# Preparing the operands of the gate and up projections in smaller pieces, placed by a time allowance on VectorE

## The chip, the cores and the metric

The kernel runs on one core of a Trainium2 chip. Its time is the device time of one execution in microseconds (us); of several runs the median is given. TensorE (PE) multiplies, VectorE (DVE) and ScalarE (ACT) work elementwise, GpSimd (POOL) and SyncE (SP) issue transfers. Each engine works through its own queue in order.

## The reference

One encoder layer: retention and windowed attention, an output projection, a LayerNorm, a SwiGLU feed-forward network with a gated embedding, and a second LayerNorm. The change is in the feed-forward network, whose matrices are 1024 x 2816 (gate, up) and 2816 x 1024 (down), for 1024 tokens in float32:

```python
h = _layer_norm(ALPHA * h + mix, ln1_gain[i], ln1_bias[i])
g = jnp.einsum('bsd,df->bsf', h, w_ffn_gate[i])
up = jnp.einsum('bsd,df->bsf', h, w_ffn_up[i])
ffn = jnp.einsum('bsf,fd->bsd', jax.nn.silu(g) * up, w_ffn_down[i])
```

## The kernel before, in words

Every float32 operand is split into a high and a low half in a reduced format (`split`, L70 to L72): ScalarE writes the high half, VectorE then subtracts it to get the low half. A product is three matmuls for each contraction tile (`mm3c`, L783 to L785): high by high, high by low, low by high.

The gate and up projections multiply 2 x 2 blocks by seven products instead of eight. The 2816 hidden columns make eleven pairs of 128-wide tiles (`Pair`, n = 0 to 10). A pair is worked through for m = 0 (gate) and m = 1 (up), and each product p of a half is one unit, written p/m below: twelve matmuls of 512 columns. Its weights are an input block or a sum of blocks (`raw` and `ln` are the loaded blocks, the sums stand in a tile named `H`), which `Pair.prep` computes and splits into one of eight operand slots (`w` and `u` tiles in the trace). The token side is prepared once for all pairs.

From pair 2 on, product 2 of both halves is taken together and is itself made of seven products of half the size, in three fine parts: F0 (products 1, 6, 5), F1 (7, 2) and F2 (4, 3), with 18, 12 and 12 matmuls of 256 columns. They share two banks, so F1 may write only when the three additions of F0's results (`post_fine`, L1295) are done. The order of units on TensorE is 1/0, 1/1, F0, 6/0, F1, 6/1, F2, 5/0, 5/1, 7/0, 7/1, 4/0, 4/1, 3/0, 3/1.

Products 1, 6, 7 and 4 of a half accumulate in one bank. Behind 1, 6 and 7 the bank is copied out by ScalarE (L1352, L1354, L1359) before the next of them may add to it. Behind 4/1 VectorE multiplies and makes three sums (L1367, L1335), behind 7 and 3 it adds (L1346), ScalarE takes the Silu (L1329) and VectorE multiplies (L1331).

All engines run in the order in which the program is written. The main loop issues unit k's matmuls, its evictions, and then `ahead(2, ...)`, which prepares operands of units up to eight further on, as long as operand slots are free:

```python
for k in range(NG):
    gunits[k][1]()
    gunits[k][2]()
    if k in (8, 11, 16, 19):
        fine.pop(0)()
    ahead(2, k + 1 + min(8, 4 + k))
```

One preparation is one piece. For product 5 it is the split and then the two sums for products 7 and 3 (L1234, L1235); for product 6 the two sums for 6 and 5 (L1227, L1228) and the split; for F0 two sums (L1243) and four splits. Slots that are short set how many preparations stand behind a unit. Loads of the next pair's weights (L1219) are issued behind the preparations of products 5 and 4.

Of the kernel before, what the change touches and what calls it, by code (L numbers as in the profile page):

```python
# [12 lines left out]
ALU = mybir.AluOpType  # L13
# [29 lines left out]
def layer(tc, xT, xn, w_first, w_mt, w_rv, w_out, w_pg, w_pe, pT, w_gu, w_dn,  # L43
          consts, dec_b, dec_c, sink, gng, lnp, out):
    nc = tc.nc
    act, dve, pool, pe, sp = nc.scalar, nc.vector, nc.gpsimd, nc.tensor, nc.sync
# [12 lines left out]
    def nm(s):  # L59
        uid[0] += 1  # L60
        return f"{s}{uid[0]}"
# [8 lines left out]
    def split(raw, hi, lo):  # L70
        act.activation(hi, raw, AF.Copy)  # L71
        dve.tensor_tensor(lo, raw, hi.bitcast(F32), ALU.subtract)  # L72
# [8 lines left out]
    def behind(ins):  # L81

        tc.add_manual_dep(ins.ins, recent[0], mybir.DependencyInfo(
            mybir.DependencyClass.NoSync, mybir.DependencyReason.DATA), reason="order")
        return ins

    last = {}
# [33 lines left out]
    def a_tile(shape, name, tag=None, dt=F32):  # L121

        turnA[0] += tag is None
        return big.tile(list(shape), dt, tag=tag or f"A{turnA[0] % 2}", bufs=4, name=nm(name))
# [8 lines left out]
    def bt(shape, tag, bufs=None, dt=F32):  # L133
        return bpool.tile(list(shape), dt, tag=tag, bufs=bufs, name=nm(tag))
# [15 lines left out]
    with tc.manual_schedule(engines={mybir.EngineType.DVE, mybir.EngineType.SP}):  # L150
        for kt in range(KT):
# [26 lines left out]
            w = wf[kt % 2]  # L178
# [81 lines left out]
    for h in range(2):  # L260
        sl = slice(h * HF, (h + 1) * HF)
        b = st[1, h]
        for g in range(2):
            a = slice(64 * g, 64 * g + 64)
# [123 lines left out]
    class Retention:  # L388


        def __init__(self, i, y, states):
            self.i, self.y, self.states = i, y, states
            self.rk, self.dq, _ = pairs[i]
            self.U = [bt([P, NT - 1, 64], f"kv{d}") for d in range(2)]
            self.kdec, self.pt, self.qq, self.r = {}, {}, {}, {}
            self.qd, self.dt = decays[i]
# [184 lines left out]
    def put(x, o, dst):  # L581
        behind(act.activation(o[:, 0, :], x, AF.Copy))
        behind(dve.tensor_tensor(o[:, 1, :], x, o[:, 0, :].bitcast(F32), ALU.subtract))
        sp.dma_start(dst, o.bitcast(F32))
# [85 lines left out]
    def ytile(k):  # L670
        if ys[k] is None:
            ys[k] = a_tile([P, S], "y", "A0" if k < 4 else "A1")
        return ys[k]
# [46 lines left out]
    with tc.manual_schedule(engines={mybir.EngineType.PE}):  # L720
# [7 lines left out]
        a = Attention(0, ytile(1))  # L728
# [11 lines left out]
        Q, X = (lambda q: (r.scores, q)), (lambda q: (r.turn, q))  # L740
# [4 lines left out]
        for i in range(1, NPAIR):  # L745
# [3 lines left out]
            a = Attention(i, ytile(2 * i + 1))  # L749
            if i == 2:  # L750
                late = [ytile(6), ytile(7)]
                op = twin(late[1].bitcast(F32R))
                side.extend(presplit_out(2, [op], 2, 3.5, late[:1]))
                side.extend(presplit_small(0, op, 30) + presplit_small(1, op, 38))
            elif i == 3:
                op = twin(bt([P, S], "aq", 3, F32R))
# [15 lines left out]
    def ct(shape, tag, bufs=None, dt=F32):  # L772
        return cpool.tile(list(shape), dt, tag=tag, bufs=bufs, name=nm(tag))
# [175 lines left out]
    part = ct([P, 8, HF], "h0b")  # L949
# [169 lines left out]
    for k in range(4):  # L1119
        c = slice(k * P, (k + 1) * P)  # L1120
# [43 lines left out]
    Q = HF // 2  # L1164
# [3 lines left out]
    oslots = []  # L1168
    fright, fsum = {}, []
# [5 lines left out]
    def take_op():  # L1175
        return oslots.pop(0)
# [32 lines left out]
    class Pair:  # L1209


        def __init__(self, n):
            self.n = n
            self.raw, self.ops, self.bank, self.ev, self.s = {}, {}, {}, {}, {}

        def load(self, m, part=(0, 1)):
            for i in part:
# [2 lines left out]
                for j in range(2):  # L1220
                    self.raw[m, i, j] = r[:, j * HF:(j + 1) * HF]

        def prep(self, p, m):
            a = lambda i, j: self.raw[m, i, j]
            s = self.s.setdefault(m, [sarena[:, 4 * m + k, :] for k in range(4)])
            if p == 6:
                dve.tensor_tensor(s[1], a(1, 0), a(1, 1), ALU.add)  # L1227
                dve.tensor_tensor(s[0], s[1], a(0, 0), ALU.subtract)  # L1228
            src = {1: lambda: a(0, 0), 2: lambda: a(0, 1), 4: lambda: a(1, 1), 5: lambda: s[1], 6: lambda: s[0],
                   7: lambda: s[2], 3: lambda: s[3]}[p]()  # L1230
            t = self.ops[p, m] = take_op()
            split(src, t[:, 0, :], t[:, 1, :])
            if p == 5:
                dve.tensor_tensor(s[2], a(0, 0), a(1, 0), ALU.subtract)  # L1234
                dve.tensor_tensor(s[3], a(0, 1), s[0], ALU.subtract)  # L1235

        def prep_fine(self, part):

            x, y = (self.raw[m, 0, 1] for m in range(2))
            left = {1: x[:, :Q], 2: x[:, Q:], 4: y[:, Q:], 5: fsum[0], 6: fsum[1], 7: fsum[2], 3: fsum[3]}  # L1240

            def sum_(q, a, b, op):
                dve.tensor_tensor(left[q], a, b, op)  # L1243

            def put(t, h, q):
                c = slice(h * Q, (h + 1) * Q)
                split(left[q], t[:, 0, c], t[:, 1, c])
                self.fine[q] = t, h * Q

            if part == 0:  # L1250
                self.fine = {}
                t, u, v = (take_op() for _ in range(3))
                self.fu = u
                sum_(5, y[:, :Q], y[:, Q:], ALU.add)
                sum_(6, left[5], x[:, :Q], ALU.subtract)
                split(x, t[:, 0, :], t[:, 1, :])
                self.fine.update({1: (t, 0), 2: (t, Q)})
                put(u, 0, 5)
                put(v, 0, 6)
            elif part == 1:  # L1260
                sum_(7, x[:, :Q], y[:, :Q], ALU.subtract)
                put(self.fu, 1, 7)
            else:
                w = take_op()
                sum_(3, x[:, Q:], left[6], ALU.subtract)
                put(w, 0, 4)
                put(w, 1, 3)

        def mm_fine(self, part):

# [110 lines left out]
    NP = NHID // 2  # L1381
    gunits = []
    pairs2 = [Pair(n) for n in range(NP)]

    def g_unit(n, p, m, k):
        pr = pairs2[n]

        def prep():
            pr.prep(p, m)
            if n + 1 < NP and p in (5, 4):  # L1390
                pairs2[n + 1].load(m, ((0,), (1,))[p == 4])

        return prep, lambda: pr.mm(p, m), lambda: pr.post(p, m, k), 1

    def f_unit(n, part):
        pr = pairs2[n]
        return lambda: pr.prep_fine(part), lambda: pr.mm_fine(part), lambda: pr.post_fine(part), (3, 0, 1)[part]

    for n in range(NP):
        for p in (1, 6, 5, 7, 4, 3) if n >= FROM else (1, 2, 6, 5, 7, 4, 3):  # L1400
# [12 lines left out]
    n = 0  # L1413
    for k, upto in enumerate((2, 4, 8, 12)):
        c = slice(k * P, (k + 1) * P)
# [35 lines left out]
    def arenas_a():  # L1451
        arena("a", rawt(2 * HF).rearrange("p (a b) -> p a b", a=2), 2)
        arena("a", rawt(2 * HF).rearrange("p (a b) -> p a b", a=2), 2)
        for _ in range(2):
            arena("a", ct([P, 2, HF], "ln", 2), 2)

    def op_arena(t, n=4):
        arena("op", t, n)
# [195 lines left out]
    dunits = []  # L1654
# [36 lines left out]

    NG, ND = len(gunits), len(dunits)
    ln2 = []
    done = [0, 0, 0]

    def ahead(what, upto):

        units = gunits if what == 2 else dunits
        while done[what] < min(upto, len(units)) and (what < 2 or units[done[2]][3] <= len(oslots)):
            units[done[what]][what % 2]()  # L1700
            done[what] += 1

    def load_ln2():
        for j in range(2):
            g = ct([P, D], "u", 4)
            sp.dma_start(g, lnp[2 + j].partition_broadcast(P))
            ln2.append(g)
# [19 lines left out]
    with tc.manual_schedule(engines={ET.PE, ET.DVE, ET.Activation, ET.Pool, ET.SP}):  # L1727
        for _ in range(4):
            oslots.append(wp.tile([P, 2, HF], F32R, tag="w", bufs=4, name=nm("w")))
            oslots.append(ct([P, 2, HF], "u", 4, F32R))  # L1730
        fine = fine_right(RIGHT[2])
        evs.extend(a_tile([P, 2, HF], "ev") for _ in range(7))
        fsum.extend([cst[:, 0:Q], cst[:, Q:2 * Q], cst[:, 2 * Q:3 * Q], ct([P, Q], "fs", 1)])
        ahead(2, 4)
        for k in range(NG):
            gunits[k][1]()
            gunits[k][2]()
            if k in (8, 11, 16, 19):
                fine.pop(0)()
            ahead(2, k + 1 + min(8, 4 + k))  # L1740
            while stores and stores[0][0] <= k:
                stores.pop(0)[1]()
            j = k + 1 - NG
            if j == -6:
                arenas_a()
                op_arena(ct([P, 4, 2, HF], "h0a", dt=F32R))
                op_arena(big16((P, 4, 2, HF)))
                op_arena(big16((P, 4, 2, HF)))
                arena("chain", ct([P, 8, HF], "h0b"), 8)
            if j == -4:  # L1750
                op_arena(big16((P, 4, 2, HF)))
                arena("b", big.tile([P, 8, HF], F32, tag="H", bufs=4, name=nm("H")), 8)
            if j >= -6:
                ahead(0, j + 7)
            if j >= -4:
                ahead(1, j + 5)
        arena("chain", ct([P, 8, HF], "h2"), 8)
        op_arena(ct([P, 4, 2, HF], "h3", dt=F32R), 4)
        rings["op"] += [ct([P, 2, HF], "u", 4, F32R) for _ in range(2)]
        for k in range(ND):  # L1760
            d_step(k)
# [85 lines left out]
```

## Time and profile before

| | us |
|---|---|
| median of 3 runs (lowest, highest) | 1214.11 (1213.49, 1217.27) |
| profiled execution | 1212.36 |
| its span, first to last instruction | 1210.6 |
| TensorE busy | 1171.8 (97%) |
| VectorE busy | 844.7 (70%) |
| ScalarE busy | 570.6 (47%) |
| gate and up stage | about 540 to 992 |

The profile lists one execution. Times are us from the span's start. A timeline row has start, length, engine, line, operation, tiles written <- read, shapes, and in brackets the idle time of the engine before it with what ended it. Each tile's buffer number is left out there. The line number is that of the code that issued the instruction, so the halves of all splits have L71 and L72, and matmuls of this stage L783 to L785. Banks are called `bmm`, `bs`, `bt` and `bo`, evicted results `ev`, the fine sums `cst` and `fs`. "Clock" is the share of TensorE's full clock that was granted.

### The profile page before, as it was taken

How to read it: one execution, taken by the hardware profiler on the slowest of the kernel's cores; microseconds unless marked ns; L12 is line 12 of the kernel's file. 1: busy time of each engine (PE TensorE's matmuls, PEld its weight loads, DVE VectorE, ACT ScalarE, POOL GpSimd, SP SyncE). 2: the span in 40 equal slices, each digit the busy share in tenths (PEclk: the TensorE clock that was granted, in tenths of full speed). 3: DMA queues.
4: the chain of work that ended last, by engine and by line, in shares of the span. 5: the costliest groups of instructions: out<-in, count | busy, mean ns of one | idle time of the engine just before them, and what ended most of it. 6: DMA issues, size and time to landing. Idle time of an engine off the chain costs nothing.

```text
span 1210.6 us, 17418 instructions
## 1 busy us (share of the span) xinstructions
PE 1171.8 (97%) x6230; PEld 975.4 (81%) x6230; DVE 844.7 (70%) x1571; ACT 570.6 (47%) x1133; POOL 120.2 (10%) x181
## 2 busy tenths in 40 slices
PE   9999999999999999999989988988998899999997
PEld 7888888888888888888878777877877788888885
DVE  5565777867758879667876667667666765765677
ACT  5665348676754364124433333334334344552463
POOL 2001021111100220000000000000000011124232
PEclk9999999999999999999999999999999999999999
DMA  7346647454457747662321241323133169999977
GB/s 253 99 155 239 232 155 266 156 191 151 155 216 248 284 173 285 206 228 82 131 98 76 87 131 62 112 88 131 44 108 109 70 186 342 355 238 212 260 172 208
DMA packets 80662, 211.73 MB, mean 175 GB/s; under 512 B 9536, under 2 KB 14784, under 8 KB 80576
## 3 DMA queue, kind: packets, MB, share of 16 engines
q1 hardware_dynamic: 71936, 193.84, 45.7%
q0 software_dynamic: 8640, 16.78, 7.9%
q8 instruction: 49, 0.80, 0.3%
q14 instruction: 37, 0.30, 0.1%
HBM read 139.29 MB, written 62.13 MB: 166 GB/s over the span
## 4 chain that ended last, share of the span: by engine, by line
PE 82%; DVE 12%; ACT 3%; issue 2%; DMA 0%; ACTq 0%; DVEq 0%; SPq 0%
PE bmm L77 6%; PE bmm L79 6%; PE bmm L78 6%; PE bt L783 5%; PE bt L785 5%; PE bt L784 5%; PE bmm L783 4%; PE bmm L785 4%; PE bmm L784 4%; PE bs L783 4%; PE bs L785 4%; PE bs L784 4%; PE bo L783 4%; PE bo L785 4%; PE bo L784 4%; DVE ev L1335 2%
## 5 line engine op out<-in xcount | busy, mean ns | idle before, releaser
L77 PE MATMUL bmm<-H,w 128*128 128x512 f32 x240 | 97.2, 405 | 0.2 <-ACT H L71 0.2
L79 PE MATMUL bmm<-H,w 128*128 128x512 f32 x240 | 94.1, 392 | 0.0
L78 PE MATMUL bmm<-H,w 128*128 128x512 f32 x240 | 94.0, 392 | 0.0
L1472 POOL DMA_DIRECT2D h0b<-in_w_dn x24 | 21.6, 902 | 576.5 <-DVE h0a L72 543.9
L72 DVE TENSOR_TENSOR w<-H,w 128x512 fp32r<-128x512 f32 x48 | 33.1, 690 | 31.9 <-ACT w L71 31.9
L77 PEld LDWEIGHTS bmm<-H,w 128*128 128x128 f32 x240 | 45.1, 188 | 10.1 <-ACT H L71 0.9
L79 PEld LDWEIGHTS bmm<-H,w 128*128 128x128 f32 x240 | 45.0, 188 | 10.0
L72 DVE TENSOR_TENSOR w<-raw,w 128x512 fp32r<-128x512 f32 x52 | 35.7, 692 | 24.4 <-ACT w L71 24.2
L78 PEld LDWEIGHTS bmm<-H,w 128*128 128x128 f32 x240 | 45.2, 188 | 7.8
L71 ACT ACTIVATE w<-H 128x512 fp32r<-128x512 f32 x48 | 30.1, 627 | 36.0 <-DVE H L1228 33.3
L71 ACT ACTIVATE u<-H 128x512 fp32r<-128x512 f32 x43 | 27.0, 628 | 41.9 <-DVE H L1228 29.6
L535 ACT ACTIVATE sc<-sc,st 128x385 f32<-128x385 f32 (+1 forms) x64 | 37.2, 585 | 17.1 <-DVE st L533 16.9
L71 ACT ACTIVATE w<-raw 128x512 fp32r<-128x512 f32 x52 | 32.1, 626 | 20.3 <-PE bmm L79 6.9
L531 DVE CUSTOM_DVE_ANT_0 sc<-cst,bs,skb 128x384 f32<-128x384 f32 (+1 forms) x64 | 34.9, 574 | 9.2 <-PE bs L530 7.9
L1329 ACT ACTIVATE ev<-ev 128x512 f32<-128x512 f32 x33 | 20.9, 633 | 36.9 <-DVE ev L1346 27.1
L72 DVE TENSOR_TENSOR u<-H,u 128x512 fp32r<-128x512 f32 x43 | 29.5, 686 | 9.4 <-ACT u L71 9.4
L72 DVE TENSOR_TENSOR u<-raw,u 128x512 fp32r<-128x512 f32 (+1 forms) x30 | 18.3, 608 | 25.4 <-ACT u L71 25.4
L541 ACT ACTIVATE sc<-sc,st 128x384 f32<-128x384 f32 (+1 forms) x64 | 34.0, 580 | 0.8 <-DVE st L539 0.8
L71 ACT ACTIVATE H<-ln 128x512 fp32r<-128x512 f32 (+1 forms) x34 | 22.9, 677 | 24.1 <-DMA ln<-ad 7.5
L526 POOL COPY sc<-skb 128x1 f32<-128x1 f32 x64 | 15.7, 253 | 182.1 <-PE bt L553 157.2
L72 DVE TENSOR_TENSOR H<-ln,H 128x512 fp32r<-128x512 f32 (+1 forms) x34 | 25.0, 746 | 8.4 <-ACT H L71 8.3
L1335 DVE TENSOR_TENSOR ev<-ev,ev 128x512 f32<-128x512 f32 x44 | 29.5, 690 | 1.1
(914 smaller groups left out, 3790.7 us busy)
## 6 DMA issues: line engine op xcount, KB each, us to landing
ad<-ev SPq DMA_DIRECT2D x33, 512.0 KB, 3.4
pgd<-pro SPq DMA_DIRECT2D x28, 512.0 KB, 3.0
raw<-in_w_gu SPq DMA_DIRECT2D x22, 512.0 KB, 4.0
ln<-in_w_gu SPq DMA_DIRECT2D x22, 512.0 KB, 4.2
raw<-ad SPq DMA_DIRECT2D x40, 256.0 KB, 5.8
ln<-ad SPq DMA_DIRECT2D x37, 256.0 KB, 6.4
H<-in_w_dn SPq DMA_DIRECT2D x33, 256.0 KB, 7.2
wod<-aq SPq DMA_DIRECT2D x15, 512.0 KB, 2.7
```

The source lines that it names most:

```text
L71: act.activation(hi, raw, AF.Copy)
L72: dve.tensor_tensor(lo, raw, hi.bitcast(F32), ALU.subtract)
L77: pe.matmul(o, lh, rh, start=start, stop=False)
L78: pe.matmul(o, lh, rl, start=False, stop=False)
L79: recent[0] = pe.matmul(o, ll, rh, start=False, stop=stop).ins.name
L531: dve.tensor_tensor_reduce(sc[g][:, :nk], cst[:, tc0:tc0 + nk], b[:, :nk], slope(i, g), skb[:, 2 * i + g:2 * i + g + 1], ALU.add, ALU.max, ...
L535: act.activation(sc[g][:, :nk + 1], sc[g][:, :nk + 1], AF.Exp, bias=st_[:, 1, j, g:g + 1], accum_out=st_[:, 2, j, g:g + 1])
L541: behind(act.activation(sc[g][:, :nk], sc[g][:, :nk], AF.Copy, scale=st_[:, 3, j, g:g + 1]))
L783: pe.matmul(o, lh, rh, start=start, stop=False, skip_group_check=True)
L784: pe.matmul(o, lh, rl, start=False, stop=False, skip_group_check=True)
L785: pe.matmul(o, ll, rh, start=False, stop=stop, skip_group_check=True)
L1335: dve.tensor_tensor(self.ev[dst][:, 0, :], left, right, op)
```

## The change

A preparation is no longer one piece. Each unit now has a list of items, and each item the number of operand slots it takes, a time for VectorE, and a function. The sums of products 6 and 5 become items of their own (`Pair.sums`), and the fine parts fall into sums, the split of the whole block and single splits; the sum for fine product 7 is made with the other sums. Each unit also carries the time of its matmuls (2.72, or 2.16, 1.44, 1.44 for the fine parts) and the time that VectorE's evictions behind it take (`after`, or 1.45). `ahead_g` puts behind unit k only items that fit in the time of unit k + 1 less the evictions of unit k and less what earlier items overdrew, except that an item of unit k + 1 always goes. The look-ahead is nine units instead of eight. Evictions, matmuls and the order of units stay.

```diff
-        def prep(self, p, m):
+        def sums(self, p, m):
             a = lambda i, j: self.raw[m, i, j]
             s = self.s.setdefault(m, [sarena[:, 4 * m + k, :] for k in range(4)])
             if p == 6:
                 dve.tensor_tensor(s[1], a(1, 0), a(1, 1), ALU.add)
                 dve.tensor_tensor(s[0], s[1], a(0, 0), ALU.subtract)
+            else:
+                dve.tensor_tensor(s[2], a(0, 0), a(1, 0), ALU.subtract)
+                dve.tensor_tensor(s[3], a(0, 1), s[0], ALU.subtract)
+
+        def prep(self, p, m):
...
             t = self.ops[p, m] = take_op()
             split(src, t[:, 0, :], t[:, 1, :])
-            if p == 5:
-                dve.tensor_tensor(s[2], a(0, 0), a(1, 0), ALU.subtract)
-                dve.tensor_tensor(s[3], a(0, 1), s[0], ALU.subtract)
...
+            def sums():
+                x, y = xy()
+                dve.tensor_tensor(fsum[0], y[:, :Q], y[:, Q:], ALU.add)
+                dve.tensor_tensor(fsum[1], fsum[0], x[:, :Q], ALU.subtract)
+                dve.tensor_tensor(fsum[2], x[:, :Q], y[:, :Q], ALU.subtract)
+
+            def whole():
+                t = take_op()
+                split(xy()[0], t[:, 0, :], t[:, 1, :])
+                f.update({1: (t, 0), 2: (t, Q)})
...
+            def last():
+                x, y = xy()
+                dve.tensor_tensor(fsum[3], x[:, Q:], fsum[1], ALU.subtract)
+                put(4, y[:, Q:])
+                put(3, fsum[3], 4)
+
+            return [[(0, 1.1, sums), (1, 0.62, whole), (1, 0.36, lambda: put(6, fsum[1])), (1, 0.36, lambda: put(5, fsum[0]))],
+                    [(0, 0.36, lambda: put(7, fsum[2], 5))], [(1, 1.1, last)]][part]
...
     def g_unit(n, p, m, k):
         pr = pairs2[n]
 
+        def sums():
+            pr.sums(p, m)
+            if n + 1 < NP and p == 5:
+                pairs2[n + 1].load(m, (0,))
+
         def prep():
             pr.prep(p, m)
-            if n + 1 < NP and p in (5, 4):
-                pairs2[n + 1].load(m, ((0,), (1,))[p == 4])
-
-        return prep, lambda: pr.mm(p, m), lambda: pr.post(p, m, k), 1
+            if n + 1 < NP and p == 4:
+                pairs2[n + 1].load(m, (1,))
+
+        items = [(1, 0.62, prep)]
+        if p == 6:
+            items.insert(0, (0, 1.24, sums))
+        elif p == 5:
+            items.append((0, 1.24, sums))
+        after = {2: (0.62, 1.24), 7: (0.62, 1.24), 4: (0, 2.5), 3: (0.62, 1.9)}.get(p, (0, 0))[m]
+        return items, lambda: pr.mm(p, m), lambda: pr.post(p, m, k), 2.72, after
 
     def f_unit(n, part):
         pr = pairs2[n]
-        return lambda: pr.prep_fine(part), lambda: pr.mm_fine(part), lambda: pr.post_fine(part), (3, 0, 1)[part]
+        return pr.prep_fine(part), lambda: pr.mm_fine(part), lambda: pr.post_fine(part), (2.16, 1.44, 1.44)[part], 1.45
...
+    items = [(u, *x) for u, g in enumerate(gunits) for x in g[0]]
+    debt = [0.0]
+
+    def ahead_g(k, upto):
+
+        units = [g[3] for g in gunits] + [2.72]
+        room = units[k + 1] - gunits[k][4] - debt[0] if k >= 0 else 100.0
+        while items and items[0][0] < upto and items[0][1] <= len(oslots) and (items[0][2] <= room or items[0][0] <= k + 1):
+            room -= items[0][2]
+            items.pop(0)[3]()
+        debt[0] = max(0.0, -room)
...
             if k in (8, 11, 16, 19):
                 fine.pop(0)()
-            ahead(2, k + 1 + min(8, 4 + k))
+                debt[0] += 2.2
+            ahead_g(k, k + 1 + min(9, 4 + k))
```

From pair 2 on the items behind each unit are the same in every pair: behind 3/0 the split of 6/0 and the last small split of F1; behind 3/1 nothing; behind 1/0 the sums and the split of 6/1; behind 1/1 F2's items and the split of 5/0; behind F0 the gate half's sums for 7 and 3; behind 6/0 the split of 5/1; behind F1 the up half's sums; behind 6/1 the splits of 7/0 and 7/1; behind F2 those of 4; behind 5/0 those of 3 and the next pair's 1/0; behind 5/1 the next 1/1 and the next fine sums; then the other fine splits one behind each of 7/0, 7/1 and 4/0, with the sums for the next 6/0 behind 4/0; behind 4/1 nothing.

On VectorE, pair 3, from F2's last small halves to F0's additions, the rows before were (`raw_5893` and `raw_5913` are the first weight blocks of the gate and up half, `w_5321` holds 5/0 and `u_5322` 5/1):

```order
L72 TENSOR_TENSOR u_5320<-fs_5337,u_5320 128x256
L72 TENSOR_TENSOR w_5321<-H_4542,w_5321 128x512
L1234 TENSOR_TENSOR H_4542<-raw_5893,ln_5973 128x512
L1235 TENSOR_TENSOR H_4542<-raw_5893,H_4542 128x512
L72 TENSOR_TENSOR u_5322<-H_4542,u_5322 128x512
L1234 TENSOR_TENSOR H_4542<-raw_5913,ln_5977 128x512
L1235 TENSOR_TENSOR H_4542<-raw_5913,H_4542 128x512
L1295 TENSOR_TENSOR ev_5336<-ev_5335,bmm_6198 128x256
L1295 TENSOR_TENSOR ev_5336<-ev_5335,bmm_6198 128x512
L1295 TENSOR_TENSOR ev_5336<-ev_5336,bmm_6198 128x256
```

The same place in the changed kernel, where L1300 is the additions, L1230 and L1231 the sums, and `raw_5931`, `raw_5965` the two blocks:

```order
L72 TENSOR_TENSOR u_5320<-fs_5337,u_5320 128x256
L72 TENSOR_TENSOR w_5321<-H_4542,w_5321 128x512
L1300 TENSOR_TENSOR ev_5336<-ev_5335,bmm_6188 128x256
L1300 TENSOR_TENSOR ev_5336<-ev_5335,bmm_6188 128x512
L1300 TENSOR_TENSOR ev_5336<-ev_5336,bmm_6188 128x256
L1230 TENSOR_TENSOR H_4542<-raw_5931,ln_6002 128x512
L1231 TENSOR_TENSOR H_4542<-raw_5931,H_4542 128x512
L72 TENSOR_TENSOR u_5322<-H_4542,u_5322 128x512
```

Four sums and the low half of 5/1 moved from in front of F0's additions to behind them.

On ScalarE, the same pair, around the copies of 1/0 and 1/1 (L1352), before (`w_5323` holds 6/0, `w_5319` 6/1, `w_5321` 5/0, `u_5318` the last fine piece of F1 and `u_5320` the two of F2):

```order
L71 ACTIVATE w_5323<-H_4542 128x512
L71 ACTIVATE u_5318<-cst 128x256
L1329 ACTIVATE ev_5333<-ev_5333 128x512
L71 ACTIVATE w_5319<-H_4542 128x512
L71 ACTIVATE u_5320<-raw_5913 128x256
L71 ACTIVATE u_5320<-fs_5337 128x256
L1352 ACTIVATE ev_5335<-bs_6157 128x512
L71 ACTIVATE w_5321<-H_4542 128x512
L1352 ACTIVATE ev_5335<-bs_6177 128x512
```

And in the changed kernel, where the copies are L1357, the Silu L1334 and the first fine piece lies in `w_5317`:

```order
L1334 ACTIVATE ev_5333<-ev_5333 128x512
L71 ACTIVATE w_5323<-H_4542 128x512
L71 ACTIVATE w_5317<-cst 128x256
L1357 ACTIVATE ev_5335<-bs_6148 128x512
L71 ACTIVATE w_5319<-H_4542 128x512
L1357 ACTIVATE ev_5335<-bs_6166 128x512
L71 ACTIVATE u_5320<-raw_5965 128x256
L71 ACTIVATE u_5320<-fs_5337 128x256
L71 ACTIVATE w_5321<-H_4542 128x512
```

The split of 6/1 moved between the two copies, and F2's two small splits, the second of which reads `fs`, moved behind both.

More of the change, by code (lines that the diff above doesn't have):

```diff
@@ L1213, in __init__ @@
             self.n = n
-            self.raw, self.ops, self.bank, self.ev, self.s = {}, {}, {}, {}, {}
+            self.raw, self.ops, self.bank, self.ev, self.s, self.fine = {}, {}, {}, {}, {}, {}
         def load(self, m, part=(0, 1)):
@@ L1228, in prep @@
                 dve.tensor_tensor(s[0], s[1], a(0, 0), ALU.subtract)
+            else:
+                dve.tensor_tensor(s[2], a(0, 0), a(1, 0), ALU.subtract)
+                dve.tensor_tensor(s[3], a(0, 1), s[0], ALU.subtract)
+        def prep(self, p, m):
+            a = lambda i, j: self.raw[m, i, j]
+            s = self.s.get(m)
             src = {1: lambda: a(0, 0), 2: lambda: a(0, 1), 4: lambda: a(1, 1), 5: lambda: s[1], 6: lambda: s[0],
@@ L1232, in prep @@
             split(src, t[:, 0, :], t[:, 1, :])
-            if p == 5:
-                dve.tensor_tensor(s[2], a(0, 0), a(1, 0), ALU.subtract)
-                dve.tensor_tensor(s[3], a(0, 1), s[0], ALU.subtract)
         def prep_fine(self, part):
[L1239 to L1243, printed above, removed]
@@ L1245, in put @@
-            def put(t, h, q):
-                c = slice(h * Q, (h + 1) * Q)
[L1247 to L1267, printed above, removed]
+            f = self.fine
@@ new lines, in xy @@
+            def xy():
+                return [self.raw[m, 0, 1] for m in range(2)]
+            def sums():
[7 more added lines that the diff above has]
+                f.update({1: (t, 0), 2: (t, Q)})
@@ new lines, in put @@
+            def put(q, src, beside=None):
+                t, h = (f[beside][0], 1) if beside else (take_op(), 0)
+                c = slice(h * Q, (h + 1) * Q)
+                split(src, t[:, 0, c], t[:, 1, c])
+                f[q] = t, h * Q
+            def last():
[5 more added lines that the diff above has]
+                    [(0, 0.36, lambda: put(7, fsum[2], 5))], [(1, 1.1, last)]][part]
@@ L1693, in layer @@
     ln2 = []
-    done = [0, 0, 0]
+    done = [0, 0]
     def ahead(what, upto):
-        units = gunits if what == 2 else dunits
-        while done[what] < min(upto, len(units)) and (what < 2 or units[done[2]][3] <= len(oslots)):
-            units[done[what]][what % 2]()
+        while done[what] < min(upto, len(dunits)):
+            dunits[done[what]][what]()
             done[what] += 1
+    items = [(u, *x) for u, g in enumerate(gunits) for x in g[0]]
[7 more added lines that the diff above has]
+        debt[0] = max(0.0, -room)
     def load_ln2():
@@ L1733, in layer @@
         fsum.extend([cst[:, 0:Q], cst[:, Q:2 * Q], cst[:, 2 * Q:3 * Q], ct([P, Q], "fs", 1)])
-        ahead(2, 4)
+        ahead_g(-1, 4)
         for k in range(NG):
```

## The prediction

> **What bounds the kernel now.** The page comes first: TensorE (PE) is busy for nearly the whole span.
>
> ```profile
> PE 1171.8 (97%) x6230; PEld 975.4 (81%) x6230; DVE 844.7 (70%) x1571; ACT 570.6 (47%) x1133; POOL 120.2 (10%) x181
> ```
>
> So only the missing 3% and the clock are to be had, and the question is where they lie. The table by stage (columns: length, then busy time of PE, PEld, VectorE (DVE), ScalarE (ACT), POOL, then granted clock, DMA share and GB/s) puts the end of pairs 0 and 1 of the gate and up stage, a steady later pair, and two pairs with a spell of halved clock beside each other:
>
> ```profile
> 569.00:611.00 42.00, 42.00 (x187) 34.74 (x186) 33.38 (x54) 17.18 (x32) 0.00 (x0) 1.00 0.28 94
> 652.40:693.80 41.40, 38.27 (x187) 32.04 (x187) 28.11 (x50) 15.28 (x28) 0.00 (x0) 1.00 0.28 95
> 693.80:736.80 43.00, 39.91 (x187) 33.25 (x187) 28.10 (x50) 15.27 (x28) 0.00 (x0) 0.96 0.28 93
> 714.30:717.70 3.40, 3.40 (x12) 2.73 (x11) 2.64 (x5) 0.87 (x2) 0.00 (x0) 0.50 0.74 261
> 861.00:904.00 43.00, 39.87 (x187) 33.23 (x186) 28.13 (x51) 15.28 (x28) 0.00 (x0) 0.96 0.28 92
> ```
>
> In the later pairs PE is idle some 3.1 us of every 41.4, while VectorE is busy for 28.1 and ScalarE for 15.3 of it: neither is short of time, so somebody's place in a queue is wrong. Line 783, the first matmul of each product, tells who is waited for (the count of 18 is 9 weight loads and 9 matmuls, one of each in the nine pairs 2 to 10):
>
> ```profile
> its engine sat idle before it (us, times) until:
>   DVE ev L1295: 48.4, 18
>   ACT ev L1352: 13.3, 18
> ```
>
> The timeline of pair 3 shows both waits, and the pace of PE without them:
>
> ```profile
> 652.23 0.39 PE L783 MATMUL bt<-h,w 128*128 128x512 f32 x1
> 654.95 0.39 PE L783 MATMUL bt<-h,u 128*128 128x512 f32 x1
> ...
> 663.11 0.28 PE L783 MATMUL bmm<-h0b,w 128*128 128x256 f32 x1
> 665.09 0.42 ACT L71 ACTIVATE u<-fs 128x256 fp32r<-128x256 f32 x1 [2.90 <-DVE fs L1243]
> 665.14 0.28 PE L785 MATMUL bmm<-sg,u 128*128 128x256 f32 x1
> 665.42 0.58 ACT L1352 ACTIVATE ev<-bs 128x512 f32<-128x512 f32 x1
> 665.89 0.62 ACT L71 ACTIVATE w<-H 128x512 fp32r<-128x512 f32 x1
> 666.05 0.50 PE L783 MATMUL bs<-H,w 128*128 128x512 f32 x1 [0.63 <-ACT ev L1352]
> ...
> 668.67 0.39 PE L785 MATMUL bs<-H,w 128*128 128x512 f32 x1
> 669.10 0.60 ACT L1354 ACTIVATE ev<-bs 128x512 f32<-128x512 f32 x1 [0.51 <-PE bs L785]
> 671.56 0.39 PE L783 MATMUL bmm<-fine,u 128*128 128x256 f32 x1 [2.50 <-DVE ev L1295]
> ```
>
> Wait A, 0.63: product 6 of the gate half (6/0) adds to the bank of 1/0, so 1/0 must be copied out first (L1352). ScalarE would copy it some 5 us earlier, but stands 2.90 behind a small split whose input `fs` VectorE has not yet computed. Wait B, 2.50: the second fine part (F1) needs the three additions L1295 of F0. F0's last matmul began at 665.14, and VectorE came to them only at 670.17, because these stood ahead of them in its queue:
>
> ```profile
> 666.55 0.69 DVE L72 TENSOR_TENSOR w<-H,w 128x512 fp32r<-128x512 f32 x1 [0.58 <-ACT w L71]
> 667.16 0.68 DVE L1234 TENSOR_TENSOR H<-raw,ln 128x512 f32<-128x512 f32 x1
> 667.76 0.69 DVE L1235 TENSOR_TENSOR H<-raw,H 128x512 f32<-128x512 f32 x1
> 668.36 0.68 DVE L72 TENSOR_TENSOR u<-H,u 128x512 fp32r<-128x512 f32 x1
> 668.96 0.68 DVE L1234 TENSOR_TENSOR H<-raw,ln 128x512 f32<-128x512 f32 x1
> 669.57 0.68 DVE L1235 TENSOR_TENSOR H<-raw,H 128x512 f32<-128x512 f32 x1
> 670.17 1.34 DVE L1295 TENSOR_TENSOR ev<-ev,bmm 128x256 f32<-128x256 f32 x3
> ```
>
> None of the six is for F1 or F2; they prepare products 5, 7 and 3, which come later. The bound is the order on VectorE, not its work.
>
> **What the waits cost.** A product of twelve 512-column matmuls takes 654.95 - 652.23 = 2.72. F0's 18 matmuls step by (665.14 - 663.11)/17 = 0.119, so F0 is 2.15, F1 and F2 (12 each) 1.43. A pair without waits is 12 x 2.72 + 2.15 + 2 x 1.43 = 37.65. The nine pairs run from the eviction of 4/1 in pair 1 to that in pair 10:
>
> ```profile
> 611.02 0.69 DVE L1367 TENSOR_TENSOR ev<-ev,bo 128x512 f32<-128x512 f32 x1
> 986.83 0.69 DVE L1367 TENSOR_TENSOR ev<-ev,bmm 128x512 f32<-128x512 f32 x1 [0.22 <-PE bmm L785]
> ```
>
> That is 375.81, and 9 x 37.65 = 338.85: 36.96 lost. Two pairs with the halved clock are 2 x (43.00 - 41.40) = 3.20 of it; the other 33.76 are 3.75 a pair, of which the rows call 3.1 idle and the rest is the drain of the pipeline before and its slow refill after each wait.
>
> The halved clock belongs to wait B. Both spells begin about 1.4 us behind one: the first at 714.3 (row above) and the other, in the window 861 to 904, at 881.6:
>
> ```profile
> 712.96 0.39 PE L783 MATMUL bs<-fine,w 128*128 128x256 f32 x1 [2.46 <-DVE ev L1295]
> 880.14 0.39 PE L783 MATMUL bs<-fine,w 128*128 128x256 f32 x1 [2.50 <-DVE ev L1295]
> 881.60:885.00 3.40, 3.40 (x10) 2.73 (x10) 2.64 (x5) 0.75 (x2) 0.00 (x0) 0.50 0.76 278
> ```
>
> I take it that a wait B now and then falls so that the clock is halved for 3.4 us, and that the spells go with the waits. [...]
>
> **The change, part by part.** The instructions are the same in kind and number; only their places on VectorE and ScalarE, and with them four loads a pair on SP, move. So nothing is to be priced but the queue, which I follow through one pair with PE at its own pace. Zero is the start of 5/0. Then 7/0 starts at 5.44, 4/1 at 13.60, 3/1 at 19.04, 1/0 at 21.76, 1/1 at 24.48, F0 at 27.20, 6/0 at 29.35, F1 at 32.07, 6/1 at 33.50, F2 at 36.22, and the pair ends at 37.65. An eviction can begin 0.20 after the product's last issue slot (669.10 - 668.67 - 0.23). VectorE and ScalarE steps come from these rows and those above:
>
> ```profile
> 655.09 0.69 DVE L1227 TENSOR_TENSOR H<-ln 128x512 f32<-128x512 f32 x1
> 655.80 0.69 DVE L1228 TENSOR_TENSOR H<-H,raw 128x512 f32<-128x512 f32 x1
> 656.61 0.63 ACT L71 ACTIVATE w<-H 128x512 fp32r<-128x512 f32 x1 [5.17 <-DVE H L1228]
> 657.28 0.69 DVE L72 TENSOR_TENSOR w<-H,w 128x512 fp32r<-128x512 f32 x1 [0.78 <-ACT w L71]
> ```
>
> One VectorE operation behind another costs 0.60 (667.16 to 667.76), or 0.71 where it needs the other's result; VectorE to ScalarE is 0.12, a ScalarE split 0.63, back to VectorE 0.04; ScalarE steps by about 0.5 (665.42, 665.89).
>
> *Wait A.* In the new ScalarE queue the copies of 1/0 and 1/1 stand ahead of the `fs` split. 1/0's copy runs from 24.7 to 25.3; 6/0 wants it at 29.35. The wait goes with 4 us to spare.
>
> *Wait B.* After 3/1 (ends 21.76) VectorE adds, multiplies by the Silu and sums: 22.1 to 24.2, allowing 0.2 for the split still in front. The two sums for 6/1 take to 25.6, its split by ScalarE to 26.4 and VectorE's half to 27.1, `fs` to 27.35. ScalarE copies 1/1 at 27.40, then splits the last fine pieces and 5/0 at 27.9, 28.25 and 28.55; VectorE's halves follow at 28.3, 28.7 and 29.2 to 29.9. F0's additions could start at 29.55, start at 29.8 and take 1.34: done at 31.2. F1 is due at 32.07. The cover is 0.9 us. The long sums for products 7 and 3 now stand behind the additions.
>
> *What is late next.* Sums for the gate half end at 32.4; 5/1 is split by 34.1; F1's additions run to 35.5 (F2 due at 36.22, and it needs only the second, done at 35.2); the other sums end at 36.75; 7/0 and 7/1 are split by 38.3 and 38.9, due 37.65 + 5.44 = 43.1 and 45.8. F2's additions start 1.0 late at 38.8, and its eight operations from there end at 43.7. The next one, for the next pair's 1/1, cannot start before 43.96 anyway, since its slot comes free only when 5/1 ends (43.1) and ScalarE splits first. So VectorE has caught up before it evicts 7/0, the round closes, and PE never waits. The least lead of any operand is the 4.8 us of 7/0.
>
> *Loads.* The first weights of the next pair's up half are now issued behind the second sums, at 36.75; they are split at 37.65 + 5.64 = 43.3. That leaves 6.5 for a landing that took, over all 512 KB loads into `raw` in the stage:
>
> ```profile
> DMA to landing us min/median/max: 3.5/4.2/5.9
> ```
>
> On SP these loads now stand behind the last store of the pair before instead of ahead of it; that store waits for the sum done at 24.2, so it holds nothing up.
>
> *Ends of the stage.* Pairs 0 and 1 have no wait now (PE is busy for 42.00 of the 42.00 from 569 to 611), and in the new order each of their preparations stands at least four products ahead of its use; the last pair leads into the down projection with the same distances. I cost both at nothing; if the cover were gone there, one or two waits of 1 us.
>
> *Sum.* The profiled execution took 1212.36 (span 1210.6 and 1.76 around it): 1212.36 - 36.96 = 1175.4. The median of the runs was 1214.11, 1.75 above the profile; one more spell of halved clock (1.6) would explain that, and should go too. So I forecast 1176 for the median, between 1175.4 and 1177.2.
>
> **Rivals.** *VectorE still late.* The allowance counts a preparation as 0.62, and one that waits for its own sum and split takes up to 2.9 in line. If VectorE is 1.9 later than I walked, F1 waits 1.0 and pays 0.3 for the refill: 9 x 1.3 = 12 and 1187. If wait A merely moves to another product, 9 x 0.9 = 8 and 1184. For: a cover of 0.9 is thin. Against: the steps come from a trace in which equal rows agree to 0.05. Chance 0.17, over 1179 to 1188.
>
> *Halved clock stays.* Then 1175.4 + 3.2 = 1178.6; chance 0.07.
>
> *The change does nothing,* because additions still wait behind other work by the tile tracking: 1212 to 1214. The order of the new kernel speaks against it. Chance 0.03.
>
> *Slower: late weights.* The up half's split stands in front of 7/0's eviction on ScalarE. With a landing L, that copy ends at 36.75 + L + 1.2, and 4/0 needs it at 48.5: PE waits once L is over 10.6, and loses more than the 4.1 it gains per pair (36.96/9) once L is over 14.7. At L = 16 it would be 1.3 x 9 = 12 slower: 1226. For: the lead on these loads falls from 12.5 us (issued behind the last sum above, which ends at 670.26) to 6.5:
>
> ```profile
> 682.76 0.63 ACT L71 ACTIVATE u<-raw 128x512 fp32r<-128x512 f32 x1 [2.09 <-PE bo L784]
> ```
>  Against: no landing in the stage exceeded 5.9. Chance 0.06.
>
> **How the numbers follow.** Forecast 0.67 (1174 to 1178), clock 0.07, late VectorE 0.17, nothing 0.03, slower 0.06. The range takes in the first three: 1173 to 1188. Faster by over 0.3% (3.6 us, about what a measurement of this kernel tells from no change): 0.91; within: 0.03; slower: 0.06.
>
> **What would show it.** Right: line 783 no longer waits for the additions or the copy; pairs are 37.65 apart; VectorE's three additions start within 0.5 us of F0's end; clock 1.00 throughout the stage. Wrong: a PE gap before F1 (VectorE late), spells of 0.50 without gaps (clock), or ScalarE idle for DMA before `raw` splits (late weights).

## The result

| | before | after |
|---|---|---|
| median of runs (lowest, highest), us | 1214.13 (1213.49, 1217.27) | 1176.52 (1176.01, 1177.20) |
| profiled execution, us | 1212.36 | 1176.84 |
| its span, us | 1210.6 | 1175.1 |

The changed kernel takes 0.9686 of the time before (95% interval 0.9668 to 0.9703), 37.6 us less. The forecast was 1176.0 in 1173 to 1188.

The page of the changed kernel, first part:

```profile
PE 1164.5 (99%) x6230; PEld 973.8 (83%) x6230; DVE 845.1 (72%) x1571; ACT 565.1 (48%) x1133; POOL 119.2 (10%) x181
```

Each engine does the same number of instructions as before. In the shorter span VectorE's and ScalarE's shares rose by one or two points, and TensorE's by two, to 99%. The table by stage, for the nine pairs with fine parts and for one of them (pair 3):

```profile
611.70:951.40 339.70, 339.70 (x1676) 288.56 (x1675) 250.28 (x445) 132.26 (x253) 1.11 (x2) 1.00 0.31 110
649.40:687.10 37.70, 37.70 (x187) 32.02 (x187) 28.07 (x51) 14.60 (x28) 0.00 (x0) 1.00 0.30 105
```

TensorE is busy in all of it, at the full clock; VectorE's 28.1 and ScalarE's 14.6 a pair now lie in 37.7 instead of 41.4. Line 783 from 611 to 1000, which showed the two waits before, has none left, so nothing stands below the two headings:

```profile
its engine sat idle before it (us, times) until:
who waited for it (us, times):
```

The timeline of pair 3 shows the two places. L1357 is the copy of 1/0 and then of 1/1, L1300 F0's additions, L1230 and L1231 the sums for products 7 and 3:

```profile
657.59 0.60 ACT L1357 ACTIVATE ev<-bs 128x512 f32<-128x512 f32 x1 [3.26 <-PE bs L785]
660.31 0.60 ACT L1357 ACTIVATE ev<-bs 128x512 f32<-128x512 f32 x1 [1.12 <-PE bs L785]
...
661.59 0.42 DVE L72 TENSOR_TENSOR u<-fs,u 128x256 fp32r<-128x256 f32 x1
662.07 0.69 DVE L72 TENSOR_TENSOR w<-H,w 128x512 fp32r<-128x512 f32 x1
662.68 1.34 DVE L1300 TENSOR_TENSOR ev<-ev,bmm 128x256 f32<-128x256 f32 x3
663.94 0.69 DVE L1230 TENSOR_TENSOR H<-raw,ln 128x512 f32<-128x512 f32 x1
664.54 0.68 DVE L1231 TENSOR_TENSOR H<-raw,H 128x512 f32<-128x512 f32 x1
...
665.01 0.28 PE L783 MATMUL bmm<-fine,w 128*128 128x256 f32 x1
```

ScalarE now waits for TensorE (3.26 and 1.12 idle, ended by PE) and copies each bank the moment it is done, where it used to wait for VectorE. VectorE's additions are done at 664.02, and F1 starts in its turn at 665.01, with no idle time before it.

### The profile page after: what moved, and what is told of

Its sections match the earlier page's. It is cut to its first block, busy times and chain, and to the rows that moved or that the text cites. A ratio compares the mean times of both kernels' runs of the same rounds, so it can differ in the third digit from the quotient of the medians.

```text
span 1175.1 us, 17378 instructions
## 1 busy us (share of the span) xinstructions
PE 1164.5 (99%) x6230; PEld 973.8 (83%) x6230; DVE 845.1 (72%) x1571; ACT 565.1 (48%) x1133; POOL 119.2 (10%) x181
## 4 chain that ended last, share of the span: by engine, by line
PE 97%; DVE 2%; ACT 1%; issue 0%; DVEq 0%; POOL 0%; POOLq 0%
PE bmm L77 6%; PE bt L783 6%; PE bt L784 6%; PE bt L785 6%; PE bmm L79 6%; PE bmm L78 6%; PE bmm L784 6%; PE bmm L783 6%; PE bmm L785 5%; PE bs L784 5%; PE bs L783 5%; PE bs L785 5%; PE bo L784 5%; PE bo L783 5%; PE bo L785 5%; PE bo L565 2%
## 5 line engine op out<-in xcount | busy, mean ns | idle before, releaser
L1334 ACT ACTIVATE ev<-ev 128x512 f32<-128x512 f32 x33 | 20.9, 632 | 74.5 <-DVE ev L1351 63.8
L72 DVE TENSOR_TENSOR u<-H,u 128x512 fp32r<-128x512 f32 x47 | 32.1, 689 | 27.9 <-ACT u L71 27.8
L72 DVE TENSOR_TENSOR w<-H,w 128x512 fp32r<-128x512 f32 x44 | 30.3, 689 | 15.2 <-ACT w L71 14.6
L72 DVE TENSOR_TENSOR u<-raw,u 128x512 fp32r<-128x512 f32 (+1 forms) x32 | 19.7, 616 | 23.5 <-ACT u L71 23.5
L71 ACT ACTIVATE w<-H 128x512 fp32r<-128x512 f32 x44 | 27.4, 622 | 8.4 <-DVE H L1228 8.4
```

## The experiments

Eight kernels were run, in two groups, and each group had its own runs of the kernel before, whose median is given with it.

### Which part of the change brings the gain

| | median, us | idle before L783, us a pair | ratio to before, 95% |
|---|---|---|---|
| before | 1214.74 | A 0.63, B 2.48 | |
| e1: the four sums moved behind the fine parts' additions | 1191.20 | A 0.61, B 0.50 | 0.981 (0.979 to 0.982) |
| e2: F2's preparation moved behind 5/0's | 1225.53 | B 3.34 | 1.009 (1.008 to 1.011) |
| e3: small pieces, no allowance | 1185.52 | B 0.73 | 0.976 (0.975 to 0.978) |
| e4: allowance, whole pieces | 1203.49 | before 5/0 1.70 | 0.991 (0.989 to 0.992) |

**e1, the sums alone.** From the kernel before:

```diff
-            if p == 5:
-                dve.tensor_tensor(s[2], a(0, 0), a(1, 0), ALU.subtract)
-                dve.tensor_tensor(s[3], a(0, 1), s[0], ALU.subtract)
...
+        post = lambda: (pr.post_fine(part), part < 2 and pr.sums(part))
...
```

> The kernel before with one thing moved from pair 2 on: the gate half's two sums for products 7 and 3 stand behind F0's additions, the up half's behind F1's; no allowance, no small pieces. (To keep the sums ahead of their use, the splits of 7 go behind those of 4, and the loads follow their last reader.) Wait A is left as it was. My theory (VectorE's queue ahead of F0's additions is wait B): those additions stand behind two splits instead of two splits and four sums and start 2.0 us earlier, so wait B falls from 2.5 to about 0.5 (its cost per pair from 2.9 to 0.9), wait A stays 0.63, no spell of halved clock: 1214 - 9 x 2.0 - 3.2 = 1193, range 1189 to 1198. Rival (the small pieces of the fine part and the allowance are what matters): no gain over 5 us, above 1209.

It took 1191.2, 23.5 less than before. The waits, for all nine pairs (18 is a weight load and a matmul each; in this kernel L1358 is the copy and L1301 the additions):

```profile
its engine sat idle before it (us, times) until:
  ACT ev L1358: 12.9, 18
  DVE ev L1301: 12.7, 18
```

Wait B fell to 0.50 and wait A stayed, as forecast. So wait B was VectorE's queue ahead of F0's additions, and moving four sums a pair in that queue (with the splits and loads that had to follow them) is worth over half of the whole gain. The rival, that the fine part's small pieces and the allowance are needed for any gain, falls.

**e2, wait A alone.** From the kernel before, the preparations of F2 and 5/0 change places:

```diff
+    preps = list(gunits)
+    for i in range(len(preps) - 1):
+        if i >= 28 and (i - 28) % 15 == 6:
+            preps[i], preps[i + 1] = preps[i + 1], preps[i]
...
```

> The kernel before with the preparation of F2 put behind that of 5/0 from pair 2 on, so that the copy of 1/0 on ScalarE no longer stands behind the split that waits for the fine sum. (The gate half's load for the next pair goes behind that of the up half's product 5.) It takes away wait A alone. My theory (A and B stand in series behind the same VectorE queue): A disappears, PE reaches F1 0.9 earlier, the additions are not a bit earlier, so wait B grows from 2.5 to about 3.3 and the pair stays 41.4; no gain, 1212 to 1216, and with gaps of 3.3 more spells of halved clock than the two of before, each 1.6, so up to 1228. Rival (A and B are independent): 9 x 0.9 = 8 faster, 1206.

It took 1225.5, 10.8 more than before, and the trace shows why. The waits of line 783, then F1's first matmul of one pair, then TensorE's clock around it:

```profile
its engine sat idle before it (us, times) until:
  DVE ev L1295: 64.1, 18
```

```profile
673.85 0.58 PE L783 MATMUL bmm<-fine,u 128*128 128x256 f32 x1 [3.34 <-DVE ev L1295]
```

```profile
672.60:679.40 6.80, 5.55 (x19) 4.97 (x20) 4.95 (x10) 1.31 (x3) 0.00 (x0) 0.50 0.54 157
```

Wait A is gone, and wait B has grown from 2.48 to 3.34, by A's 0.63 and most of the 0.26 that a wait costs besides (below): the two stood one behind the other in front of the same queue, and taking away the first only lets TensorE arrive earlier at the second. Each of the nine waits now has a spell of halved clock, four of them of twice the length, as in the last row (6.80 us at 0.50); the mean clock of the profiled execution is 0.980, where before's is 0.995. That is the loss: without a spell a pair would take 41.35 (37.74 without waits, 3.34, and 0.27 for the restart), against 41.40 before. The time lies above the 1212 to 1216 of the theory and inside its "up to 1228" for more spells. The rival that A and B are independent falls.

**e3, pieces without the allowance.** In the changed kernel:

```diff
-        room = units[k + 1] - gunits[k][4] - debt[0] if k >= 0 else 100.0
+        room = 100.0
```

> The changed kernel with the room always 100: small pieces, placed by free slots and look-ahead alone. Walked through by hand as in the prediction: the sums for 6/1 move ahead of 3/0's eviction, but the splits of 5/0 and 5/1 and all four sums for 7 and 3 stand ahead of F0's additions again; these end at 33.0 instead of 31.2, F1 is due at 32.1: wait B of about 1.0, no wait A, no spells; 9 x 1.3 = 12 above the changed kernel: 1188, range 1183 to 1196. Rival (small pieces alone bring the gain): 1176 to 1178. Rival (the allowance is all of it): 1205 or more.

It took 1185.5. Between the copies and F0's additions VectorE's queue is the old one again, only begun earlier:

```profile
661.75 0.69 DVE L72 TENSOR_TENSOR w<-H,w 128x512 fp32r<-128x512 f32 x1 [0.58 <-ACT w L71]
662.36 0.68 DVE L1230 TENSOR_TENSOR H<-raw,ln 128x512 f32<-128x512 f32 x1
662.96 0.68 DVE L1231 TENSOR_TENSOR H<-raw,H 128x512 f32<-128x512 f32 x1
663.56 0.69 DVE L72 TENSOR_TENSOR u<-H,u 128x512 fp32r<-128x512 f32 x1
664.17 0.69 DVE L1230 TENSOR_TENSOR H<-raw,ln 128x512 f32<-128x512 f32 x1
664.77 0.69 DVE L1231 TENSOR_TENSOR H<-raw,H 128x512 f32<-128x512 f32 x1
665.37 1.34 DVE L1300 TENSOR_TENSOR ev<-ev,bmm 128x256 f32<-128x256 f32 x3
...
666.77 0.38 PE L783 MATMUL bmm<-fine,w 128*128 128x256 f32 x1 [0.72 <-DVE ev L1300]
```

The wait was forecast at 1.0 and is 0.72. Small pieces let the sums for 6/1 go ahead of 3/0's eviction, so all of it starts earlier, and the copy of 1/0 too, which ends wait A. That alone brings 29 of the 38 us, by another way than e1; the allowance brings about the last 9. Both rivals fall. The look-ahead of nine units is the same in e3 and e4 as in the changed kernel, and its own share was not tried.

**e4, the allowance with whole pieces.** In the changed kernel:

```diff
         if p == 6:
-            items.insert(0, (0, 1.24, sums))
+            items = [(1, 1.86, lambda: (sums(), prep()))]
         elif p == 5:
-            items.append((0, 1.24, sums))
+            items = [(1, 1.86, lambda: (prep(), sums()))]
```

and F0's preparation becomes one item of 2.44.

> The changed kernel with the allowance kept, but the pieces whole again: product 5's split and its sums one item of 1.86, product 6's sums and split one of 1.86, F0's preparation one of 2.44. The 1.86 of 5/0 then fits nowhere between 1/1 and F2, so 5/0 is split only behind F2's additions, immediately before its use. By my walk waits A and B are gone, but PE waits about 2.8 for 5/0's operand once a pair: 9 x 3.0 = 27 above the changed kernel, 1203, range 1197 to 1210 with some spells of halved clock. Rival (the allowance alone brings the gain, the grain does not matter): 1176 to 1180.

It took 1203.5, where 1203 was expected, though the parts differ. The end of 1/1 and the start of 5/0 on TensorE in one pair, and then the clock behind them:

```profile
672.59 0.28 PE L785 MATMUL bmm<-h0b,u 128*128 128x256 f32 x1
674.57 0.50 PE L783 MATMUL bo<-H,w 128*128 128x512 f32 x1 [1.70 <-ACT w L71]
674.90 0.40 PE L784 MATMUL bo<-H,w 128*128 128x512 f32 x1
675.38 0.68 PE L785 MATMUL bo<-H,w 128*128 128x512 f32 x1
```

```profile
675.60:678.90 3.30, 3.30 (x9) 2.56 (x9) 3.30 (x7) 1.71 (x4) 0.00 (x0) 0.50 0.30 77
```

TensorE waits for 5/0's operand as forecast, but 1.7 instead of 2.8: I had let the first matmul wait for both halves, and it needs only the high half, which ScalarE writes. The third one, which reads the low half, waits another quarter of a us (674.90 to 675.38, where steps are 0.23). Five of the nine waits brought a spell of halved clock (mean clock of the profiled execution 0.990), more than I had allowed for, and made up the difference; it is luck that the time came out as forecast. What follows is that the allowance alone starves TensorE: a piece of 1.86 fits behind none of the units from 1/1 to 6/1, so 5/0 is split only when it is due.

### How much cover the new order has, and what halves the clock

Here one or more operations were put ahead of F0's additions in the changed kernel:

```diff
             if part == 0:
+                r, h = self.raw, self.s[0][2]
+                for _ in range(1):
+                    dve.tensor_tensor(h, r[0, 0, 0], r[0, 1, 0], ALU.subtract)
                 add(c12, v[:, 0, Q:], bx)
```

> The changed kernel with one more VectorE operation in each pair from 2 on, right ahead of F0's additions: the first of the gate half's sums for 7 and 3, made once more than needed (the result is the same). It shifts the additions by 0.60. My theory: F1 was released 0.9 before its turn, so 0.60 is covered and nothing is lost, 1176 to 1177, no PE gap, no spell. Rival (VectorE's work itself bounds the stage now): 9 x 0.6 = 5 slower, 1182.

> The same with two such operations. They write the same tile one behind the other, so the shift is 0.60 + 0.72 = 1.32, of which 0.9 is covered. My theory: F1 waits 0.2 to 0.3 in the rows and the pair loses 0.26 more for the refill of the pipeline (e1 and e3 lost 0.26 a wait beyond their idle time), 9 x 0.5 = 4.5: 1181, range 1180 to 1183, no spell. Rival (VectorE's work bounds): 9 x 1.32 = 12, 1188.

> The same with four, a shift of 0.60 + 3 x 0.72 = 2.76: F1 waits about 1.7 in the rows. My theory: 9 x (1.7 + 0.26) = 17.5 for the waits, 1194 without spells; and since e4 had five spells at waits of 1.69, one to six spells of 1.6 each, on a grid of 3.413 us: 1195 to 1204. [...]

> The same with five, a shift of 3.48: F1 waits about 2.4, close to the 2.5 of the kernel before, but without wait A. My theory: 9 x (2.4 + 0.26) = 24 for the waits, 1200.5, and two to six spells of 1.6 each: 1203 to 1211. Rival (the spells of the kernel before came from something else that the change took away): 1200 to 1201 and a clock of 1.00 throughout the stage.

The kernel before took 1213.00 in the runs of e5 to e8; the first row is the changed kernel of the result, whose runs of the kernel before gave 1214.13.

| operations (shift, us) | median, us | idle before F1, us | spells in the profile |
|---|---|---|---|
| none | 1176.52 | 0 | 0 |
| 1 (0.60), e5 | 1177.22 | 0 | 0 |
| 2 (1.32), e6 | 1181.50 | 0.23 | 0 |
| 4 (2.76), e7 | 1194.41 | 1.68 | 0 |
| 5 (3.48), e8 | 1206.19 | 2.42 | 4 |

The rows of line 783 for e6, e7 and e8, in this order:

```profile
  DVE ev L1300: 8.0, 18
  DVE ev L1300: 34.1, 18
  DVE ev L1300: 47.3, 18
```

F1 of one pair, first in e7, then in e8:

```profile
668.16 0.38 PE L783 MATMUL bmm<-fine,w 128*128 128x256 f32 x1 [1.68 <-DVE ev L1300]
...
672.44 0.58 PE L783 MATMUL bmm<-fine,w 128*128 128x256 f32 x1 [2.42 <-DVE ev L1300]
```

The clock of the stage (1.00 and 0.98, third number from the end), in the same order:

```profile
611.70:985.00 373.30, 358.13 (x1746) 301.10 (x1746) 287.77 (x503) 139.77 (x267) 6.34 (x7) 1.00 0.33 110
...
611.70:1000.00 388.30, 366.54 (x1758) 308.65 (x1757) 295.60 (x513) 140.10 (x268) 6.35 (x7) 0.98 0.32 107
```

VectorE did more work in all four, and nothing was lost until the cover was used up: 0.60 is free (e5's pairs take 37.74, as without it), 1.32 is not. So VectorE's work does not bound the stage; what counts is when F0's additions start. The waits of e6, e7 and e8 fit the walk to 0.1 us. The forecast of e7 failed: I had expected one to six spells and 1195 to 1204, there are none, and 1194.41 is what the waits alone had been reckoned at (1194). In e8, one operation longer, the wait is 2.42, nearly as long as in the kernel before (2.46 to 2.50), and the spells are back, four of them. The rival of e8, that the change removed the spells in some other way than by the waits, falls with e8 and e2.

## Why the prediction was right

**The bound.** Right. The two waits were VectorE's and ScalarE's order and not their work: e1 and e3 shorten wait B by order alone, e5 adds work without loss, e2 shows that A and B stood in series.

**The walk.** Its zero, the start of 5/0 in the pair before, lies at 632.88 in the trace after, the start of this row:

```profile
632.88 0.40 PE L783 MATMUL bt<-H,w 128*128 128x512 f32 x1
```

The copy of 1/0 was forecast at 24.7 and began at 24.71. F0's additions were forecast from 29.8 to 31.2 and ran from 29.80 to 31.14; F1 was due at 32.07 and came at 32.13, so the cover is 1.0 instead of 0.9, and e5 and e6 bracket it between 0.60 and 1.32. The gate half's sums end at 32.3 (forecast 32.4), read from L1231 above. The rest of the round holds as well: the other sums end at 36.76 (forecast 36.75), F2's additions start at 38.87 (38.8) and the eight operations from there end at 43.69 (43.7). The stage runs as it was followed by hand.

**The sum.** 1175.4 was forecast for the profiled execution and 1176.84 measured. The two ends of the nine pairs:

```profile
611.69 0.69 DVE L1372 TENSOR_TENSOR ev<-ev,bo 128x512 f32<-128x512 f32 x1
...
951.35 0.69 DVE L1372 TENSOR_TENSOR ev<-ev,bmm 128x512 f32<-128x512 f32 x1 [0.28 <-PE bmm L785]
```

That is 339.66, or 37.74 a pair, where the forecast had 37.65. The 0.09 lies at the three places of a pair where a product follows a fine part: 6/0 takes 2.75 there (662.26 to 665.01), not 2.72:

```profile
662.26 0.40 PE L783 MATMUL bs<-H,w 128*128 128x512 f32 x1
662.50 0.40 PE L784 MATMUL bs<-H,w 128*128 128x512 f32 x1
662.73 0.39 PE L785 MATMUL bs<-H,w 128*128 128x512 f32 x1
```

The pace of a product had been taken from one that follows another product; the first step here is 0.24 instead of 0.23, and the next ones are slow too. Nine pairs make 0.8 of the miss. Another 0.67 lies ahead of the nine pairs, where this execution was later (611.69 against 611.02). It was already 0.77 later at line 783's very first matmul, at 358.88 against 358.11; in the ten profiles that place ranges from 358.11 to 359.50, so this is spread between executions. That the median, 1176.52, came within 0.5 of its forecast of 1176 is in part luck: the forecast put the median 0.6 above the profiled execution, and it lies 0.3 below.

**The clock.** That the halved clock belongs to wait B, and goes with it, was an inference from two spells; e2 and e8 bear it out. So does the step from the profile to the median: of the eleven runs of the kernel before that went with e1 to e8, those of mean clock 0.995 took 1212.5 to 1213.3, those of 0.994 took 1213.7 to 1214.7 and those of 0.991 took 1216.8 and 1216.9, while four runs after, at 0.998, lie within 1.2 us. With the spells left in place the profiled execution was reckoned at 1178.6; the stage ran at 1.00 throughout and took 1176.84, while gaps of 2.42 to 2.50 brought spells in e8 and before. The grid on which the forecast of e7 puts its spells is shown by no run: the two spells of the kernel before last 3.4 us each, at a clock of 0.50, and begin 167.25 apart (714.30 and 881.55), which is too few for a grid, and e7 had none.

**The rivals.** VectorE late: no, though its thin cover is real. Late weights: no. The 512 KB loads into `raw`, though issued later, took at most 3.9 us to land, where they took up to 5.9 before (the 2.5 is a smaller load for the down projection). Below that line stand the first matmul behind 5/1 and the split that the forecast feared for:

```profile
DMA to landing us min/median/max: 2.5/3.5/3.9
```

```profile
676.09 0.39 PE L783 MATMUL bs<-H,u 128*128 128x512 f32 x1
676.11 0.63 ACT L71 ACTIVATE u<-raw 128x512 fp32r<-128x512 f32 x1 [0.68 <-ACT w L71]
```

It starts at 676.11, right as TensorE goes on from 5/1 to the next product, which is when 5/1's slot comes free; its row names no DMA as what ended the wait. How far the loads may slip was not tried.

## What to carry to other kernels

Where the busiest engine waits though its servants are idle for a third of the time, look at what stands ahead of the awaited instruction in its engine's queue, and move only that: four sums a pair moved were worth 24 us here, while one wait removed alone made the kernel slower, because the next wait in the same queue absorbed it and, grown from 2.48 to 3.34, came with a halved clock nine times in nine instead of twice. Preparations should be cut so small that they fit behind the evictions of a unit, and be given out by time rather than by free buffers; either of the two alone left some of the gain on the table, 9 us without the allowance and 27 without the small pieces. Following the new order through one period by hand, with steps read from the old trace, was accurate to about 0.1 us.

## What was not expected of the hardware

*Waits cost more than their rows say.* Each wait of TensorE lost about 0.26 beyond its idle time, at 0.23 as at 2.42: e6's pair is 38.24 for 37.74 + 0.23, e7's 39.68 for 37.74 + 1.68, e8's without a spell 40.43 for 37.74 + 2.42, each between F1's starts in successive pairs. The rows of e7 show where it goes, on both sides of its F1 above (668.16):

```profile
666.09 0.39 PE L785 MATMUL bs<-H,w 128*128 128x512 f32 x1
...
668.38 0.28 PE L784 MATMUL bmm<-fine,w 128*128 128x256 f32 x1
```

The last row before the wait lasts 0.39, but the next matmul would have followed 0.23 after its start, so the idle time is counted 0.16 too short; and the first step behind the wait is 0.22 (668.16 to 668.38) instead of 0.12. e4's pair, with a second pause behind the first, lost 0.60 beyond its idle time (40.04 for 37.74 + 1.70).

*In these ten profiles the length of a wait alone does not tell whether the clock is halved behind it.* The waits of each kernel in the stage, nine of each length, and how many of them had a spell:

| | idle before, us | waits with a spell | mean clock of the profiled execution |
|---|---|---|---|
| e2 | 3.34 | nine, four of twice the length | 0.980 |
| before | A 0.63, B 2.46 to 2.50 | two, both behind B | 0.995 |
| e8 | 2.42 | four | 0.993 |
| e4 | 1.70, and 0.25 two matmuls later | five | 0.990 |
| e7 | 1.68 | none | 0.998 |
| e3 | 0.73 | none | 0.998 |
| e1 | A 0.61, B 0.50 | none | 0.998 |
| e6 | 0.23 | none | 0.998 |
| after, e5 | 0 | none | 0.998 |

All nine waits of 3.34 had a spell, and none of 1.68 or less. In between the count does not follow the length: e8's waits are a little shorter than those of the kernel before and had twice as many spells, and e4's 1.70, with its second pause, had five where e7's 1.68 had none. What decides which of nine nearly equal waits has a spell was not shown.
